# Gate products of a gated hybrid decoder layer as 2 by 2 blocks with seven products

## The chip, the cores and the metric

The kernel runs on one core of a Trainium2 chip. The metric is the device time of one execution in microseconds (us), the median of several runs. TensorE (PE; its weight loads are listed as PEld) multiplies, VectorE is DVE, ScalarE is ACT, GpSimd is POOL, and SyncE (SP) issues most DMAs.

## The reference

One layer of a decoder runs over N = 544 tokens (512 of a prompt, 8 x 4 of samples), with 1024 channels. After a modulated norm, `h` goes through one projection whose columns feed three token mixers and three gates:

```python
h = _rmsnorm(x, lp["norm1_g"]) * (1.0 + sc1) + sh1
z = h @ lp["w_in"]
xa, q, k, v, u, gates = jnp.split(z, list(IN_SPLITS), axis=-1)
...                       # ya: pooling mixer, yb: windowed attention, yc: S5 state space mixer (SSM)
ga, gb, gc = jnp.split(jax.nn.sigmoid(gates), N_BRANCH, axis=-1)
merged = ga * (ya @ lp["w_branch_a"]) + gb * (yb @ lp["w_branch_b"]) + gc * (yc @ lp["w_branch_c"])
x = x + g1 * (merged @ lp["w_out"])
h2 = _rmsnorm(x, lp["norm2_g"]) * (1.0 + sc2) + sh2
a_up, b_up = jnp.split(h2 @ lp["w_ffn_in"], 2, axis=-1)
x = x + g2 * ((jax.nn.silu(a_up) * b_up) @ lp["w_ffn_out"])
```

Each gate is a 1024 by 1024 product. The change concerns the gates `gb` and `gc`.

## The kernel before

All activations lie transposed: a tile holds 128 channels by 544 tokens, so `h` is eight such tiles. Every fp32 operand of a large product is split into a rounded part and a remainder (`hi`, `lo`), and a product is three passes: weight `hi` by `h` hi, weight `hi` by `h` lo, weight `lo` by `h` hi. `quarter` (line 663) splits four weight tiles of 128 x 128 at once: ACT copies into `whi`, DVE subtracts into `wlo`. There are four buffers of each. `gemm` (line 681) runs the three passes for each of the k tiles, each pass as two matmuls of 272 columns (H2 = 272 is half of N).

The three branches follow one another. The eight gate tiles of the first branch are made early (`tgs`, line 763); `mix` (line 1038) multiplies a gate tile by a branch tile's product and adds it to `merged` on POOL for the second and third branch. `branch` (line 1052) does the second and third: for each of four pairs of column tiles it loads 256 gate columns (`load_g`) and 256 branch columns into two of three `raw` buffers, and then does gate, mix, gate, mix; a gate tile is 48 matmuls (`gate`, line 751: 8 k tiles, 3 passes, 2 halves), a mix 24. After the first gate of some pairs comes an `ada` block (line 546), which has two more raw loads of 1 MB, 8 matmuls, a copy and 4 transposes. Between the second and third branch stands the SSM's GLU (line 1079).

The FFN's pairs (`pair`, line 1261) already compute a pair of tiles by a 2 by 2 block scheme: with the weights cut into `a0`, `a1`, `b0`, `b1` (two column tiles by two halves of the channels) and `h2` into halves of channels and of tokens, seven products of 4 k tiles x 3 passes of 272 columns (`product`) replace eight. They need four sums of weight blocks (`s1` to `s4`, tag `ux`) and four sums of blocks of the activation (`T1` to `T4`), which are made once, on DVE and ACT, from the eight `gf` tiles that the FFN's norm leaves. Seven of the sixteen tiles of these sums lie in a large buffer (`tsum`, tag `T`, one buffer), nine in ordinary slots.

That buffer of tag `T` holds first raw weights, then the SSM's taps (`ssm.T`, read by `outputs`), then these sums. Of ordinary slots of 128 x 544 there are 56 (`NS`).

The order of the work is made by a planner (`Program.run`, line 181) before the kernel is built. Each operation has an estimated cost and a priority, which is its place in the program, lowered by a million within `P.high()`. At each moment an engine takes the ready operation of lowest number whose tiles fit (`fits`, line 210: a tile may be taken only if all tiles of lower number that are still to come would have room too). The result is one fixed order for each engine; at run time each engine goes through its own and waits on semaphores.

Of the kernel before, what the change touches and what calls it, by code (L numbers as in the profile page):

```python
# [10 lines left out]
F32 = mybir.dt.float32  # L11
F32R = mybir.dt.float32r
AF = mybir.ActivationFunctionType
OP = mybir.AluOpType
# [416 lines left out]
def body(tc, I, O, dbg=None):  # L431
# [4 lines left out]
    with ExitStack() as ctx:  # L436
# [314 lines left out]
        def gate(b, m, rg):  # L751
            wg = split_w(rg[:, :, 128 * (m % 2):128 * (m % 2) + 128], KT)
            ps = mmt()
            gemm(ps, wg, h1, KT)
            tg = st([128, N], "tg")
            with P.high():
                S.activation(h2v(tg), pv_(ps), AF.Tanh, scale=0.5)
            return tg
# [268 lines left out]
        def split_a(src, name, scale=None):  # L1027
            hi = st([128, N], name + "h", F32R)
            lo = st([128, N], name + "l", F32R)
            if scale is None:  # L1030
                S.copy(hi, src)
                V.tensor_tensor(lo, src, hi.bitcast(F32), op=OP.subtract)
            else:
                S.activation(hi, src, AF.Copy, scale=scale)
                V.scalar_tensor_tensor(lo, src, scale, hi.bitcast(F32), op0=OP.mult, op1=OP.subtract)
            return hi, lo

        def mix(b, m, rb, y, tg):
            wb = split_w(rb[:, :, 128 * (m % 2):128 * (m % 2) + 128], 4)
            ps = mmt()  # L1040
            gemm(ps, wb, y, 4)
            if b == 0:
                mt = st([128, N], "merged")
                merged.append(mt)
            else:
                mt = tg
            with P.high():
                V.scalar_tensor_tensor(h2v(mt), h2v(tg), 1.0, pv_(ps), op0=OP.add, op1=OP.mult)
            if b:
                G.tensor_tensor(merged[m], merged[m], tg, op=OP.add)  # L1050

        def branch(b, y, load, blks):
            for m2 in range(4):
                rg, rb = load_g(b, m2), load(m2)
                for m in (2 * m2, 2 * m2 + 1):
                    tg = gate(b, m, rg)
                    if m == 2 * m2 and m2 < len(blks):
                        ada(blks[m2])
                    mix(b, m, rb, y, tg)

        for m2 in range(4):
            rb = load_w(I["w_branch_a"][0, :, 256 * m2:256 * m2 + 256], 4, 256)
# [3 lines left out]
        def load_b(m2):  # L1066
# [4 lines left out]
                             I["w_branch_b"][0, 256 * h:256 * h + 256, 256 * m2:256 * m2 + 256].rearrange("(k p) n -> p k n", p=64))  # L1071
            return v

        yb = [split_a(ybT[t], "yb") for t in range(4)]
        ssm.stage2()
        branch(1, yb, load_b, (4, 5, 8, 9))


# [171 lines left out]
            V.tensor_tensor(h2v(f), h2v(sg), pv_(pss[1]), op=OP.mult)  # L1250
            return split_a(f, "ff")

        def product(ps, w, act, start):
            for k in range(4):
                (wh, wl), (ah, al) = w[k], act[k]
                with P.unit():
                    for j, (a, b) in enumerate(((wh, ah), (wh, al), (wl, ah))):
                        PE.matmul(ps, a, b, start=start and k == 0 and j == 0, stop=k == 3 and j == 2,
                                  skip_group_check=True)

        def pair(i):

            raw = raw_tile()
            a, b = (raw[:, 1024 * j:1024 * j + 1024].rearrange("p (k n) -> p k n", k=KT) for j in range(2))
            for j, v in enumerate((a, b)):
                c0 = 2816 * j + 128 * i
                SY.dma_start(v, w_ff[:, c0:c0 + 128].rearrange("(k p) n -> p k n", p=128))
            a0, a1, b0, b1 = a[:, 0:4], a[:, 4:8], b[:, 0:4], b[:, 4:8]
            pb, pa_, pd = aux()[:, :H2], mmt()[:, 0, :H2], aux()[:, :H2]
            part, u3, c = st([128, 2, H2], "part"), st([128, 2, H2], "u3"), st([128, N], "ff")  # L1270
            cl, cr = c[:, t0], c[:, t1]
            product(pb, quarter(a0), X00, True)
            with P.high():
                S.copy(part[:, 0], pb)
            product(pa_, quarter(a1), X10, True)
            with P.high():
                V.tensor_tensor(cl, pa_, part[:, 0], op=OP.add)
                S.activation(cl, cl, AF.Silu)
            s1, s2, s3, s4 = (P.tile(up, [128, 4, 128], F32, "ws", "ux", 4) for _ in range(4))
            with P.high():  # L1280
                V.tensor_tensor(s1, b0, b1, op=OP.add)
                V.tensor_tensor(s2, s1, a0, op=OP.subtract)
            product(pb, quarter(s2), T2, False)
            with P.high():
                S.copy(part[:, 1], pb)
            product(pd, quarter(s1), T1, True)
            with P.high():
                V.tensor_tensor(s3, a0, b0, op=OP.subtract)
            product(pb, quarter(s3), T3, False)
            with P.high():  # L1290
                S.copy(u3[:, 0], pb)
                V.tensor_tensor(u3[:, 0], pd, u3[:, 0], op=OP.add)
            product(pb, quarter(b1), T4, False)
            with P.high():
                V.tensor_tensor(s4, a1, s2, op=OP.subtract)
            product(pd, quarter(s4), X11, False)
            with P.high():
                V.tensor_tensor(cr, pd, part[:, 1], op=OP.add)
                V.tensor_tensor(cl, cl, pb, op=OP.mult)
                S.activation(cr, cr, AF.Silu)  # L1300
            V.tensor_tensor(cr, cr, u3[:, 0], op=OP.mult)
            return split_a(c, "ff")

        last = len(PARTS) - 1
        plain = [plain_pair(i) for i in range(2)]


        t0, t1 = slice(0, H2), slice(H2, N)
        room = P.tile(up, [128, 7, N], F32R, "tsum", "T", 1)
        homes = [room[:, i] for i in range(7)]  # L1310

        def home(name):
            return homes.pop() if homes else st([128, N], name, F32R)

        T13, T42 = [], []
        for k in range(4):
          with P.high():
            ga, gb = gfs[k], gfs[k + 4]
            V.tensor_tensor(ga[:, t0], ga[:, t1], ga[:, t0], op=OP.subtract)
            V.tensor_tensor(ga[:, t1], gb[:, t1], ga[:, t1], op=OP.subtract)  # L1320
            V.tensor_tensor(gb[:, t1], gb[:, t1], ga[:, t0], op=OP.subtract)
            V.tensor_tensor(gb[:, t0], gb[:, t0], gb[:, t1], op=OP.subtract)
            for g, dst in ((ga, T13), (gb, T42)):
                hi, lo = home("th"), home("tl")
                S.copy(hi, g)
                V.tensor_tensor(lo, g, hi.bitcast(F32), op=OP.subtract)
                dst.append((hi, lo))
        cols = lambda ps, sl: [(hi[:, sl], lo[:, sl]) for hi, lo in ps]
        X00, X10, X11 = cols(hh[0:4], t0), cols(hh[4:8], t0), cols(hh[4:8], t1)
        T1, T3, T4, T2 = cols(T13, t0), cols(T13, t1), cols(T42, t0), cols(T42, t1)  # L1330

        for part, FH in enumerate(PARTS):
            ff = plain if part == 0 else []
# [458 lines left out]
```

## Time and profile before

| what | value |
|---|---|
| median of 3 runs | 940.92 us (940.81 to 941.09) |
| the profiled execution, in all | 939.36 us |
| its span, first to last instruction | 937.6 us |
| mean granted TensorE clock | 0.988 of full speed |
| instructions in the span | 17684 |
| second branch to the last mix of the third | about 312 to 479 us of the span |
| pairs of the FFN | from about 578 us on, between products of its second matrix |

Times in the rows below are microseconds from the start of the span unless marked ns. In a group of instructions, `out<-in` names the written and read tiles, followed by their shapes, the count, the total busy time and the mean of one. "aux" and "mm" are accumulators in PSUM. In the chain that ended last, each row is a stretch of work that set the end, or the time from it to the next. All lines carry the number of one helper (L426), so tile names tell where a row belongs.

### The profile page before, as it was taken

Reading aid. Unit: us, or ns where it says so; the run is one execution under the profiler, and the core shown is the slowest. Engines: PE = TensorE matmul, PEld = TensorE weight load, DVE = VectorE, ACT = ScalarE, POOL = GpSimd, SP = SyncE. Lnnn points to the kernel's source line nnn. Section 1 sums busy time; section 2 is a strip of 40 time slices with the busy share of each in tenths; the row PEclk is TensorE's granted clock in tenths of the full one; section 3 lists DMA queues with packets and bytes.
Section 4 is the critical chain, followed back from the end, with each engine's and each line's share of the span. In section 5 each row is a group of like instructions: output and inputs, shape, how many; then the busy total and the mean of one; then the engine's idle time right before and its main releaser. Section 6 shows DMA issues by size and latency. Waiting matters only on the chain.

```text
span 937.6 us, 17684 instructions
## 1 busy us (share of the span) xinstructions
PE 895.0 (95%) x7112; PEld 836.6 (89%) x7112; DVE 571.8 (61%) x1226; ACT 409.7 (44%) x871; POOL 105.4 (11%) x126
## 2 busy tenths in 40 slices
PE   2999999999999999999999999999999999999996
PEld 1698998898969998999999879999999999999996
DVE  5468788755663322433336689874578874588743
ACT  6346333345373222332343465652255552155554
POOL 3001000255630011101111100000000000000020
PEclk9799999999998999999999999999999999999998
DMA  9781422600211555544353361323523223432122
GB/s 290 252 258 51 124 79 74 162 24 24 94 30 46 157 158 172 188 157 158 110 190 122 119 166 45 92 63 94 158 80 100 70 67 92 135 92 63 57 63 96
DMA packets 128079, 107.16 MB, mean 114 GB/s; under 512 B 4058, under 2 KB 110942, under 8 KB 127973
## 3 DMA queue, kind: packets, MB, share of 16 engines
q1 hardware_dynamic: 127453, 105.50, 37.5%
q8 instruction: 56, 0.92, 0.4%
q0 software_dynamic: 448, 0.48, 0.3%
q14 instruction: 26, 0.21, 0.1%
q10 hardware_dynamic: 96, 0.04, 0.0%
HBM read 102.39 MB, written 4.81 MB: 114 GB/s over the span
## 4 chain that ended last, share of the span: by engine, by line
PE 82%; DVE 8%; DMA 4%; ACT 3%; issue 1%; SPq 1%; DVEq 0%; ACTq 0%
PE mm L426 55%; PE aux L426 27%; DVE wlo L426 2%; DMA cb<-in_ssm_b_re_dram 1%; ACT whi L426 1%; DVE ffl L426 1%; SPq L426 1%; DVE gf L426 1%; DMA spn<-in_state_pool_dram 1%; DMA xtok<-in_x_prompt_dram 1%; DMA raw<-in_w_ffn_in_dram 1%; DVE Hst L426 0%; DVE rm L426 0%; DVE ws L426 0%; DVE vv L426 0%
## 5 line engine op out<-in xcount | busy, mean ns | idle before, releaser
L426 ACT CAST whi<-raw 128x512 fp32r<-128x512 f32 x224 | 137.2, 614 | 251.0 <-PE mm L426 202.2
L426 DVE TENSOR_TENSOR wlo<-raw,whi 128x512 fp32r<-128x512 f32 x224 | 160.1, 716 | 109.4 <-ACT whi L426 107.2
L426 PE MATMUL mm<-hh,whi 128*128 128x272 f32 x608 | 135.4, 304 | 0.0
L426 PE MATMUL mm<-hl,whi 128*128 128x272 f32 x608 | 126.2, 289 | 0.0
L426 PE MATMUL mm<-hh,wlo 128*128 128x272 f32 x608 | 126.0, 288 | 0.0
L426 PEld LDWEIGHTS mm<-hh,whi 128*128 128x128 f32 x608 | 95.0, 189 | 13.8 <-issue 11.0
L426 PEld LDWEIGHTS mm<-hl,whi 128*128 128x128 f32 x608 | 95.8, 189 | 0.0
L426 PEld LDWEIGHTS mm<-hh,wlo 128*128 128x128 f32 x608 | 95.7, 189 | 0.0
L426 ACT CAST whi<-ws 128x512 fp32r<-128x512 f32 x80 | 48.8, 619 | 66.5 <-PE aux L426 51.1
L426 PE MATMUL mm<-ffh,whi 128*128 128x272 f32 x328 | 68.2, 289 | 0.0
L426 PE MATMUL mm<-ffh,wlo 128*128 128x272 f32 x328 | 67.8, 288 | 0.0
L426 PE MATMUL mm<-ffl,whi 128*128 128x272 f32 x328 | 67.6, 287 | 0.0
L426 POOL TENSOR_TENSOR ssq<-ssq,sq 128x544 f32<-128x544 f32 x10 | 13.6, 1360 | 422.6 <-ACT sq L426 422.6
L426 DVE TENSOR_TENSOR wlo<-ws,whi 128x512 fp32r<-128x512 f32 x80 | 54.4, 687 | 8.5 <-ACT whi L426 5.6
L426 DVE SCALAR_TENSOR_TENSOR xback<-mm,modT,xback 128x272 f32<-128x272 f32 (+3 forms) x64 | 28.4, 478 | 50.8 <-PE mm L426 50.8
L426 PE MATMUL aux<-tsum,whi 128*128 128x272 f32 x280 | 59.2, 292 | 0.0
L426 PE MATMUL aux<-tl,whi 128*128 128x272 f32 x200 | 57.6, 288 | 0.0
L426 PE MATMUL aux<-ghi,wlo 128*128 128x272 f32 x160 | 47.6, 297 | 4.8 <-DVE wlo L426 4.7
L426 PEld LDWEIGHTS mm<-ffl,whi 128*128 128x128 f32 x328 | 51.4, 188 | 0.0
L426 PEld LDWEIGHTS mm<-ffh,wlo 128*128 128x128 f32 x328 | 51.3, 188 | 0.0
L426 PEld LDWEIGHTS mm<-ffh,whi 128*128 128x128 f32 x328 | 51.3, 188 | 0.0
L426 PE MATMUL aux<-ghi,whi 128*128 128x272 f32 x160 | 46.1, 288 | 0.0
(412 smaller groups left out, 2097.2 us busy)
## 6 DMA issues: line engine op xcount, KB each, us to landing
raw<-in_w_ada_dram SPq DMA_DIRECT2D x23, 1024.0 KB, 8.9
raw<-in_w_ffn_in_dram SPq DMA_DIRECT2D x44, 512.0 KB, 4.8
raw<-in_w_in_dram SPq DMA_DIRECT2D x16, 1024.0 KB, 6.4
raw<-in_w_ffn_out_dram SPq DMA_DIRECT2D x16, 512.0 KB, 3.8
raw<-in_w_out_dram SPq DMA_DIRECT2D x4, 1024.0 KB, 5.5
raw<-in_w_ffn_out_dram SPq DMA_DIRECT2D x8, 384.0 KB, 3.5
xtok<-in_x_prompt_dram SPq DMA_DIRECT2D x8, 256.0 KB, 6.5
T<-gd SPq DMA_DIRECT2D x32, 64.0 KB, 3.3
```

The source lines that it names most:

```text
L426: return p.add(tag, cost, lambda: fn(*a, **k), ins, writes, fset, nbytes, after, lock)
```

## The change

In the second and third branch, seven of the eight pairs of gate tiles are computed by the seven products; the first pair of the second branch stays as it was, though its two gates now both come before its two mixes. `product` and the body of `pair` become shared functions (`product`, `seven`), and the sums of the activation a function `sums`, called for `h1` (`XH`, ahead of the second branch, at ordinary priority; it first rebuilds fp32 tiles by adding hi and lo) and for the FFN (`XG`, as before). The sums of `h` take the buffer of tag `T` after the SSM's taps, and nine slots. Each new pair has both gates, then the `ada` block, then both mixes.

```diff
@@ -1052,11 +1052,18 @@
         def branch(b, y, load, blks):
             for m2 in range(4):
                 rg, rb = load_g(b, m2), load(m2)
-                for m in (2 * m2, 2 * m2 + 1):
-                    tg = gate(b, m, rg)
-                    if m == 2 * m2 and m2 < len(blks):
-                        ada(blks[m2])
-                    mix(b, m, rb, y, tg)
+                if b == 1 and m2 == 0:
+                    tg, u3 = gate(b, 0, rg), gate(b, 1, rg)
+                else:
+                    tg, pb, u3 = seven(rg[:, 0:4, 0:128], rg[:, 4:8, 0:128], rg[:, 0:4, 128:256], rg[:, 4:8, 128:256], XH,
+                                       AF.Tanh, 0.5, "tg")
+                    with P.high():
+                        S.activation(u3[:, t0], pb, AF.Tanh, scale=0.5)
+                        S.activation(u3[:, t1], u3[:, t1], AF.Tanh, scale=0.5)
+                if m2 < len(blks):
+                    ada(blks[m2])
+                mix(b, 2 * m2, rb, y, tg)
+                mix(b, 2 * m2 + 1, rb, y, u3)
 
         for m2 in range(4):
             rb = load_w(I["w_branch_a"][0, :, 256 * m2:256 * m2 + 256], 4, 256)
@@ -1071,8 +1078,87 @@
                              I["w_branch_b"][0, 256 * h:256 * h + 256, 256 * m2:256 * m2 + 256].rearrange("(k p) n -> p k n", p=64))
             return v
 
+        t0, t1 = slice(0, H2), slice(H2, N)
+        def sums(full, act):
+            room = P.tile(up, [128, 7, N], F32R, "tsum", "T", 1)
+            homes = [room[:, i] for i in range(7)]
+            def home(name):
+                return homes.pop() if homes else st([128, N], name, F32R)
+            T13, T42 = [], []
+            for k in range(4):
+              with P.shift(0 if full is None else -10 ** 6):
+                if full is None:
+                    ga, gb = (st([128, N], "xsum") for _ in range(2))
+                    for g, (hi, lo) in ((ga, act[k]), (gb, act[k + 4])):
+                        V.tensor_tensor(g, hi.bitcast(F32), lo.bitcast(F32), op=OP.add)
+                else:
+                    ga, gb = full[k], full[k + 4]
+                V.tensor_tensor(ga[:, t0], ga[:, t1], ga[:, t0], op=OP.subtract)
+                V.tensor_tensor(ga[:, t1], gb[:, t1], ga[:, t1], op=OP.subtract)
+                V.tensor_tensor(gb[:, t1], gb[:, t1], ga[:, t0], op=OP.subtract)
+                V.tensor_tensor(gb[:, t0], gb[:, t0], gb[:, t1], op=OP.subtract)
+                for g, dst in ((ga, T13), (gb, T42)):
+                    hi, lo = home("th"), home("tl")
+                    S.copy(hi, g)
+                    V.tensor_tensor(lo, g, hi.bitcast(F32), op=OP.subtract)
+                    dst.append((hi, lo))
+            cols = lambda ps, sl: [(hi[:, sl], lo[:, sl]) for hi, lo in ps]
+            return {"X00": cols(act[0:4], t0), "X10": cols(act[4:8], t0), "X11": cols(act[4:8], t1),
+                    "T1": cols(T13, t0), "T3": cols(T13, t1), "T4": cols(T42, t0), "T2": cols(T42, t1)}
+        def product(ps, w, act, start):
+            for k in range(4):
+                (wh, wl), (ah, al) = w[k], act[k]
+                with P.unit():
+                    for j, (a, b) in enumerate(((wh, ah), (wh, al), (wl, ah))):
+                        PE.matmul(ps, a, b, start=start and k == 0 and j == 0, stop=k == 3 and j == 2,
+                                  skip_group_check=True)
+        def seven(a0, a1, b0, b1, X, func, scale, name):
+            pb, pa_, pd = aux()[:, :H2], mmt()[:, 0, :H2], aux()[:, :H2]
+            part, u3, c = st([128, 2, H2], "part"), st([128, N], "u3"), st([128, N], name)
+            cl, cr, ur = c[:, t0], c[:, t1], u3[:, t1]
+            product(pb, quarter(a0), X["X00"], True)
+            with P.high():
+                S.copy(part[:, 0], pb)
+            product(pa_, quarter(a1), X["X10"], True)
+            with P.high():
+                V.tensor_tensor(cl, pa_, part[:, 0], op=OP.add)
+                S.activation(cl, cl, func, scale=scale)
+            s1, s2, s3, s4 = (P.tile(up, [128, 4, 128], F32, "ws", "ux", 4) for _ in range(4))
+            with P.high():
+                V.tensor_tensor(s1, b0, b1, op=OP.add)
+                V.tensor_tensor(s2, s1, a0, op=OP.subtract)
+            product(pb, quarter(s2), X["T2"], False)
+            with P.high():
+                S.copy(part[:, 1], pb)
+            product(pd, quarter(s1), X["T1"], True)
+            with P.high():
+                V.tensor_tensor(s3, a0, b0, op=OP.subtract)
+            product(pb, quarter(s3), X["T3"], False)
+            with P.high():
+                S.copy(ur, pb)
+                V.tensor_tensor(ur, pd, ur, op=OP.add)
+            product(pb, quarter(b1), X["T4"], False)
+            with P.high():
+                V.tensor_tensor(s4, a1, s2, op=OP.subtract)
+            product(pd, quarter(s4), X["X11"], False)
+            with P.high():
+                V.tensor_tensor(cr, pd, part[:, 1], op=OP.add)
+                S.activation(cr, cr, func, scale=scale)
+            return c, pb, u3
         yb = [split_a(ybT[t], "yb") for t in range(4)]
         ssm.stage2()
+        XH = sums(None, h1)
         branch(1, yb, load_b, (4, 5, 8, 9))
 
 
@@ -1250,14 +1336,6 @@
             V.tensor_tensor(h2v(f), h2v(sg), pv_(pss[1]), op=OP.mult)
             return split_a(f, "ff")
 
...
         def pair(i):
 
             raw = raw_tile()
@@ -1265,69 +1343,16 @@
             for j, v in enumerate((a, b)):
                 c0 = 2816 * j + 128 * i
                 SY.dma_start(v, w_ff[:, c0:c0 + 128].rearrange("(k p) n -> p k n", p=128))
...
+            c, pb, u3 = seven(a[:, 0:4], a[:, 4:8], b[:, 0:4], b[:, 4:8], XG, AF.Silu, 1.0, "ff")
             cl, cr = c[:, t0], c[:, t1]
-            product(pb, quarter(a0), X00, True)
             with P.high():
...
                 V.tensor_tensor(cl, cl, pb, op=OP.mult)
-                S.activation(cr, cr, AF.Silu)
-            V.tensor_tensor(cr, cr, u3[:, 0], op=OP.mult)
+            V.tensor_tensor(cr, cr, u3[:, t1], op=OP.mult)
             return split_a(c, "ff")
 
         last = len(PARTS) - 1
         plain = [plain_pair(i) for i in range(2)]
-
-
...
+        XG = sums(gfs, hh)
 
         for part, FH in enumerate(PARTS):
             ff = plain if part == 0 else []
```

Left out are the lines of `pair` that `seven` now holds word for word, and those of the FFN's sums that `sums` now holds.

## Rows read from the trace of the kernel before

**Rows 1.** The page: busy time by engine; chain that ended last, by engine.
```profile
PE 895.0 (95%) x7112; PEld 836.6 (89%) x7112; DVE 571.8 (61%) x1226; ACT 409.7 (44%) x871; POOL 105.4 (11%) x126
...
PE 82%; DVE 8%; DMA 4%; ACT 3%; issue 1%; SPq 1%; DVEq 0%; ACTq 0%
```

**Rows 2.** Chain that ended last, in the branches: start, length, what.
```profile
333.41 3.20 PE mm L426 x24
...
337.60 1.71 PE mm L426 x12
...
354.32 3.20 PE mm L426 x24
...
435.36 43.74 PE mm L426 x348
```

**Rows 3.** Windows: busy time (instructions) of each engine, granted clock, DMA.
```profile
core 0: us, PE busy (x) PEld busy (x) DVE busy (x) ACT busy (x) POOL busy (x), PEclk, DMA share, GB/s
284.00:292.00 8.00, 8.00 (x51) 7.09 (x50) 0.72 (x1) 1.60 (x7) 0.00 (x0) 0.71 0.00 0
292.00:312.00 20.00, 20.00 (x157) 19.45 (x156) 11.71 (x19) 7.71 (x14) 0.00 (x0) 0.96 0.23 64
312.40:333.40 21.00, 21.00 (x169) 18.99 (x165) 5.93 (x11) 5.31 (x10) 3.04 (x2) 1.00 0.61 178
...
588.85:599.97 11.12, 10.81 (x85) 10.59 (x85) 9.54 (x17) 6.50 (x15) 0.00 (x0) 1.00 0.35 94
```

**Rows 4.** Chain that ended last, in the FFN's pairs.
```profile
588.85 4.53 PE aux L426 x34
...
597.94 0.62 ACT whi L426
...
598.59 0.72 DVE ffl L426
599.31 0.61 DVE wlo L426
...
599.97 4.52 PE aux L426 x34
```

**Rows 5.** Chain that ended last: the product into mm, two FFN pairs apart.
```profile
718.34 1.51 PE mm L426 x12
...
740.76 1.51 PE mm L426 x12
```

**Rows 6.** Groups by shape over the span: busy us, mean ns, idle before.
```profile
L426 DVE TENSOR_TENSOR wlo<-raw,whi 128x512 fp32r<-128x512 f32 x218 | 157.6, 725 | 108.7 <-ACT whi L426 106.5 <-PE aux L426 1.1
...
L426 ACT CAST whi<-raw 128x512 fp32r<-128x512 f32 x218 | 134.8, 619 | 247.1 <-PE mm L426 200.1 <-PE aux L426 23.1 <-ACT part L426 7.5
...
L426 DVE TENSOR_TENSOR wlo<-ws,whi 128x512 fp32r<-128x512 f32 x80 | 54.4, 687 | 8.5 <-ACT whi L426 5.6
...
L426 DVE TENSOR_TENSOR ws<-raw 128x512 f32<-128x512 f32 x40 | 27.3, 689 | 0.8
...
L426 DVE TENSOR_TENSOR ffl<-ff,ffh 128x544 fp32r<-128x544 f32 x22 | 15.8, 719 | 0.1
...
L426 DVE SCALAR_TENSOR_TENSOR tg<-tg,mm 128x544 f32<-128x544 f32 x16 | 11.5, 721 | 39.0 <-PE mm L426 39.0
...
L426 DVE TENSOR_TENSOR ff<-aux,part 128x272 f32<-128x272 f32 x20 | 8.7, 436 | 1.5 <-PE aux L426 1.5
```

**Rows 7.** Matmuls on the taps: ns min/median/max, first and last start.
```profile
L426 PE MATMUL aux<-T,U x64: 272/273/273, 124.0 to 189.1; 128*72 128x128 f32 x64
```

**Rows 8.** SP's queue in the second branch, in order of time.
```profile
330.56 0.37 SPq L426 DMA_DIRECT2D raw<-in_w_ada_dram  x1
333.47 0.37 SPq L426 DMA_DIRECT2D raw<-in_w_in_dram  x1
```

**Rows 9.** POOL in order of time, around 379.
```profile
379.32 1.35 POOL L426 TENSOR_TENSOR merged<-merged,tg 128x544 f32<-128x544 f32 x1 [8.50 <-DVE tg L426]
```

**Rows 10.** DVE in order of time, around 379.
```profile
379.62 1.61 DVE L426 TENSOR_TENSOR wlo<-raw,whi 128x512 fp32r<-128x512 f32 x1 [0.38 <-ACT whi L426]
```

More of the change, by code (lines that the diff above doesn't have):

```diff
@@ L1251, in plain_pair @@
             return split_a(f, "ff")
[L1253 to L1259, printed above, removed]
         def pair(i):
@@ L1267, in pair @@
                 SY.dma_start(v, w_ff[:, c0:c0 + 128].rearrange("(k p) n -> p k n", p=128))
-            a0, a1, b0, b1 = a[:, 0:4], a[:, 4:8], b[:, 0:4], b[:, 4:8]
-            pb, pa_, pd = aux()[:, :H2], mmt()[:, 0, :H2], aux()[:, :H2]
-            part, u3, c = st([128, 2, H2], "part"), st([128, 2, H2], "u3"), st([128, N], "ff")
+            c, pb, u3 = seven(a[:, 0:4], a[:, 4:8], b[:, 0:4], b[:, 4:8], XG, AF.Silu, 1.0, "ff")
             cl, cr = c[:, t0], c[:, t1]
-            product(pb, quarter(a0), X00, True)
             with P.high():
[L1274 to L1298, printed above, removed]
                 V.tensor_tensor(cl, cl, pb, op=OP.mult)
-                S.activation(cr, cr, AF.Silu)
-            V.tensor_tensor(cr, cr, u3[:, 0], op=OP.mult)
+            V.tensor_tensor(cr, cr, u3[:, t1], op=OP.mult)
             return split_a(c, "ff")
@@ L1305, in body @@
         plain = [plain_pair(i) for i in range(2)]
[L1308 to L1330, printed above, removed]
+        XG = sums(gfs, hh)
         for part, FH in enumerate(PARTS):
```

## The prediction

> **What bounds the kernel now.** I read the page's busy shares first and then the chain that ended last [rows 1]: TensorE is busy for 95% of the span and carries 82% of the chain. A busy TensorE proves little by itself, so the next view is the chain in the stretch that the change touches, the second and third branch [rows 2]. There the chain is TensorE without a hole. Its last unbroken piece holds 348 matmuls of 272 columns in 43.74 us, 43.74 / 348 = 0.1257 us each. From 333.41 to 354.32 one turn of the second branch (two gate tiles of 48 matmuls, two mixes of 24, one `ada` block) takes 20.91 us; 144 x 0.1257 = 18.10, so the `ada` block costs 2.81 and nothing is left for waiting. The windows [rows 3] show the other engines in the same stretch: DVE 5.93 of 21.0 us, ACT 5.31, POOL 3.04, and the granted clock at 1.00, its upper level of 2.4 GHz. So a matmul that is left out here is worth its 0.1257 us, if the weights and sums that replace it come in time.
>
> The nearest thing to the new code runs already: the FFN's pairs do the same seven products. Their chain [rows 4] shows what that costs. A pair has 7 x 12 = 84 matmuls, 84 x 0.1257 = 10.56 us, but comes every 11.12 us (588.85 to 599.97). The missing 0.56 is one chain per pair: a weight buffer comes free, ACT makes `whi`, DVE finishes an `ffl`, then makes `wlo`, and only then does the next product go on. Later in the FFN two pairs take 740.76 - 718.34 = 22.42 us [rows 5], a loss of 22.42 / 2 - 10.56 = 0.65 each. In that stage DVE is 86% busy (9.54 of 11.12) [rows 3].
>
> **The change, part by part.**
>
> *Matmuls removed.* Seven pairs of gate tiles go from 96 to 84 matmuls of the same width and the same count of passes: 7 x 12 = 84 fewer, 84 x 0.1257 = -10.56 us. Nothing is added on TensorE; the mixes, the `ada` blocks and the loads have the same sizes.
>
> *DVE work added in a pair* [rows 6]. Three more `wlo` (0.73 from raw, 0.69 from sums), four weight sums `ws` at 0.69, and three adds out of PSUM at 0.44. The whole of DVE in a new pair: 3 x 0.73 + 4 x 0.69 for `wlo`, 4 x 0.69 for `ws`, 3 x 0.44, two `wlo` (1.45) and two `tg` (1.44) of the mixes: 11.9 us, with the `mgl` of the third branch (priced as an `ffl`, 0.72) 13.4. TensorE's part of that pair is 84 + 48 = 132 matmuls, 16.6 us, and 19.4 with an `ada` block. So DVE stays below TensorE as a mean, at 72 to 81% without the `ada`, a little under the FFN's 86%.
>
> *ACT work added.* Three more `whi` at 0.62, three copies and four half activations in place of two full ones. ACT was busy for 5.31 of 21.0 us; twice that is still under two thirds. I cost it at nothing; it counts only as the first link of the FFN's stall.
>
> *The stall inside a pair.* The third product into `pb` must be copied out by ACT before the fourth may go on adding to it, and the next weight buffer is freed late, as in the FFN. Something else must fill TensorE there. Where an `ada` block lies behind the pair (five of the seven), its matmuls read raw weights and need no split, so they can fill it; in the other two the first mix has to, and its `wlo` comes by the same route as in the FFN. From below the stall is 0 (the gate stretch today has none), from above 0.65 (the FFN). I take 0.64 for the two and 0.15 for the five, nearer to zero because no `ffl` stands ahead of `wlo` and a filler exists: 2 x 0.64 + 5 x 0.15 = +2.0 us. Bounds 0 and 7 x 0.65 = 4.6.
>
> *The sums of h.* `sums(None, h1)` costs DVE 8 adds of 544 columns, 16 of 272 and 8 `lo` of 544: 8 x 0.72 + 16 x 0.44 + 8 x 0.72 = 18.6 us [rows 6], and ACT 8 copies. The first pair that uses them is the second of branch two, around 333, and its first two products need no sum. Their big buffer is the one of the SSM's taps, whose last reader runs at 189.1 [rows 7]. What holds them back are the 56 slots: by my count of the tiles alive they fit once the first branch's tiles go, from some point between 285 and 296. DVE has room from there: 7.3 free of 8 us (284 to 292), 8.3 of 20, and 12.0 of 21 in the untouched first pair even after POOL's 3.04 is taken off as if it blocked DVE [rows 3]. That is 27.6 us for 18.6, so most is hidden; I put +0.3. If the cover before 312 were gone, 18.6 - 12.0 = 6.6 would show; with no cover at all, 18.6.
>
> *Slots.* Nine slots stay taken through both branches: 16 (h) + 8 (merged) + 8 + 4 + 9 = 45 of 56. A pair needs three and `ada` one, so pairs still run. Splits for the GLU, now made early, must wait for the end of branch two. They are off the chain, and the next gate needs none of them; 0, at most 8 `lo` at 0.72 = 5.8 if TensorE had to stand behind them.
>
> *Loads.* The gate's raw tile is held until the last weight sum, some 8 us into the pair, and both mixes come after it. Today one raw buffer of the three is handed on just in time: `w_in` is issued at 333.47 [rows 8], after the first half of the `ada` block, and its gate runs from 337.60, covered by one mix and half an `ada`, some 4 us. After the change two mixes (6.0 us) lie in that place. I cost it at 0.
>
> *FFN.* The same products through the shared function; one multiply is issued after an activation instead of before it: 0.
>
> Sum against the profiled execution (span 937.6, 939.36 in all, that is 1.76 around the span): 939.36 - 10.56 + 2.0 + 0.3 = 931.1 us. The median of the runs is 940.92, 1.56 above that execution, so the forecast is 932.6 us; its own range, with stalls from 0 to 3.5 and the sums at up to 0.5, is 930.4 to 934.4.
>
> **One rule against it.** When POOL's add of `merged` ran from 379.32 for 1.35 us, a `wlo` that began at 379.62 took 1.61 us instead of 0.69 [rows 9, 10]. The Trainium skill (SBUF — State Buffer, "SBUF: two separate sides") says that a DVE instruction with two SBUF inputs and a GpSimd instruction share a port pair that whoever starts first locks for its whole length; the trace agrees. `wlo` and `ws` are of that kind, and there are more of them now: by that rule the fourteen adds of the seven pairs could hold DVE for 14 x 1.35 = 18.9 us, where the sum above goes by today's chain, in which the blocked `wlo` cost TensorE nothing, and puts 0.
>
> **Rivals.**
> - *A, the FFN's stall everywhere.* Seven times 0.65, with 1 to 2 us of the sums showing because DVE runs them beside the splits. For it: the same function, the same four weight buffers. Against: 48 of the 132 matmuls of a pair are mixes, in which DVE has little to do. 940.92 - 10.56 + 4.6 + 1 to 2 = 936 to 937.
> - *B, POOL's adds stop the splits.* Two adds per pair now follow each other within 3 us of mixes, just when the next pair's first weights are split. If one add of 1.35 per pair shows on TensorE: 932.6 + 7 x 1.35 = 942.1, no change. With 11.9 + 2 x 1.35 = 14.6 of 16.6 us (16.1 in the third branch) DVE would nearly be the bound. Against: today the same blockings cost TensorE nothing.
> - *C, slower: the sums are not covered.* The third product of the first new pair needs all four tiles of T2. If the slots let the sums begin only behind the untouched pair, 18.6 us stand open: 932.3 + 18.6 = 950.9. It decides from 8.6 us in the open (940.92 - 932.3).
> - That the change removes less than it says is ruled out by the counts: every product is 12 matmuls of 272 columns.
>
> **How the numbers follow.** Forecast 0.60, A 0.21, B 0.08, C 0.09; 0.02 is left for something not seen. A measurement of this kernel tells about 0.2%, 1.9 us, from no change. The forecast and A are faster: 0.81. B and a C just at its point are the same: 0.09; slower 0.10. The range runs from no stall at all (930.4, with the scatter of the runs 930.2) to A's end with some of the slots' cost, 937.8; it holds the forecast and A.
>
> **What the profile would show.** TensorE has 7028 matmul records, DVE some 100 more (70 in the pairs, 32 in the sums), ACT some 64 more. The chain between 312 and the output projection stays TensorE, with holes of 0.3 to 0.6 us in the pairs without `ada`, released by DVE `wlo`; wide holes in every pair speak for A, holes behind `wlo` of 1.3 us or more beside POOL for B. The `th` and `tl` sums are done before about 336; a TensorE hole there, released by DVE, is C. The stretch from 312.5 to 479.1 shrinks by 8 us, and everything after it, the FFN above all, keeps its length. I am wrong if a stage outside the branches moves by more than 1 us: then the order of the plan, not this sum, decided.

## The result and the profile after

The changed kernel takes 934.33 us (median of five runs, 932.29 to 935.95) against 940.92 before on the same chip: a ratio of 0.9935, 95% interval 0.9915 to 0.9954, that is 6.1 us faster with an interval of 4.3 to 8.0. On another chip it was 935.05 against 940.63, 0.9942 (0.9923 to 0.9961), 5.5 us. The forecast of 932.6 was 1.7 to 2.5 us too low; the range of 930.2 to 937.8 held it. The profiled execution took 935.95 us (span 934.0), the longest of its five.

First, the page: busy time by engine, and the chain that ended last by engine.

```profile
PE 889.2 (95%) x7028; PEld 828.5 (89%) x7028; DVE 634.8 (68%) x1328; ACT 435.3 (47%) x935; POOL 107.8 (12%) x126
...
PE 82%; DVE 7%; DMA 5%; ACT 4%; SPq 1%; issue 1%; DVEq 0%; ACTq 0%
```

Against [rows 1], 84 matmuls are gone and 102 DVE and 64 ACT instructions have come, as forecast. TensorE's share of the chain is unchanged. What is new is DMA with 5% for 4%, in a kernel that loads nothing more.

To see where the time went I cut each span at points that every variant has, all read from matmuls of one kind: the first on `yah` (begin of the branches' mixes), the last on `yah` (the first branch is done), the first on `xagain` (the last mix is done, output projection), `ghi` on `wth` (begin of the FFN), `ffh` on `whi` (first product with the FFN's second matrix) and `ffh` on `wth` (its last part), to the end of the span. "Branches" runs from the first `yah` to `xagain`; "behind yah" is the part of it that follows the last `yah`. In us:

```
                                  branches  behind yah  out. projection  FFN, begin  FFN, rest  tail
before                              227.6      173.8          57.5           96.1       281.7    23.3
after                               219.7      163.5          59.4           97.2       282.1    23.2
after, other chip                   219.6      163.3          59.1           97.2       282.1    23.3
order alone (e1)                    228.2      172.0          57.4           96.0       282.0    23.3
nine slots held (e2)                230.0      173.8          57.6           96.0       282.1    23.4
second branch only (e3)             224.8      168.8          57.4           96.4       281.9    23.3
third branch only (e4)              221.7      168.0          58.6           97.2       282.1    23.3
half of x in a raw tile (e7)        217.0      163.3          57.6           97.4       282.0    23.2
  the same, other chip              218.1      163.3          57.6           97.2       282.0    23.3
before, half of x in raw (e7b)      230.0      173.8          57.4           95.9       282.5    23.4
w_out loads behind x (e9)           219.8      163.7          57.5           97.2       282.0    23.5
sums twice on DVE (e6)              232.6      176.3          59.4           97.2       281.9    23.3
all eight pairs (e5)                234.0      169.9          60.4           97.0       281.8    23.3
```

So the branches gave 7.9 us, and two stages that the sum had at nothing took 3.0 back. What lies ahead of the branches differs by up to 4 us from profile to profile (250.3 to 254.6 us, with the time at which the first taps have landed), whatever the variant; I read nothing from it.

**The granted clock in the branches' first part.** These are windows of after (busy us of each engine with its instructions, granted clock, DMA's share, GB/s); the first two lie in the first branch, whose matmuls the change leaves as they were, the last covers a new pair of the second.

```profile
core 0: us, PE busy (x) PEld busy (x) DVE busy (x) ACT busy (x) POOL busy (x), PEclk, DMA share, GB/s
284.00:288.00 4.00, 4.00 (x18) 3.54 (x18) 0.82 (x2) 0.41 (x2) 0.00 (x0) 0.50 0.00 0
288.00:292.00 4.00, 4.00 (x26) 3.41 (x24) 0.00 (x0) 0.00 (x0) 0.00 (x0) 0.50 0.00 0
...
332.50:351.90 19.40, 19.40 (x154) 17.43 (x154) 12.08 (x19) 9.72 (x20) 3.43 (x2) 1.00 0.64 191
```

From 284 to 292 the granted clock is 0.50, the lower level of 1.2 GHz, where [rows 3] has 0.71; the matmuls there are the same ones in the same order. Summing (1 - granted clock) x 4 us over 276 to 304 gives 6.8 us lost after and 3.4 before. But e2 and e7b, whose branches hold before's work, lost 6.8 as well and took 230.0 us; e4 lost 3.4, and the same kernel e7 lost 3.4 in one profile and 5.1 in another. It is an execution's luck, worth 230.0 - 227.6 = 2.4 us in this stretch. The unprofiled runs of before on the second chip show as much: five at a mean granted clock of 0.988 took 938.8 us on average, six at 0.984 took 941.0. Against e2 and e7b, which have after's clock, after's branches gave 230.0 - 219.65 = 10.35 us. The part behind `yah`, where the granted clock is 1.00 in before and after alike, says the same without them: 173.8 in before, e2 and e7b, 163.5 and 163.3 after.

**The pairs.** The chain that ended last, in after (start, length, what):

```profile
342.94 1.72 PE mm L426 x12
...
357.46 0.95 PE mm L426 x6
...
362.39 1.70 PE mm L426 x12
...
440.16 1.51 PE mm L426 x12
...
446.15 0.62 ACT whi L426
446.78 0.29 ACT u L426
...
447.11 3.27 PE aux L426 x24
...
457.16 1.51 PE mm L426 x12
...
467.02 8.49 DMA xagain<-in_x_prompt_dram
```

One new pair with its `ada` block and two mixes takes 362.39 - 342.94 = 19.45 us; before it was 20.91 [rows 2]. The chain there is TensorE alone, but not at its full rate: the six mix matmuls at 357.46, which stand where the copy out of `pb` is awaited, take 0.95 us for 6 x 0.1257 = 0.75. At 446.1 the chain leaves TensorE inside a pair, the only time between 300 and 466: the fourth product into `pb` waits for ACT to copy the third one out (`u`), and that copy stood behind a `whi`. The last line is new and belongs to the output projection.

### The profile page after: what moved, and what is told of

Same layout as the page of the kernel before. It is cut to its first block, busy times and chain, and to the rows that moved or that the text cites. A ratio compares the mean times of both kernels' runs of the same rounds, so it can differ in the third digit from the quotient of the medians.

```text
span 934.0 us, 17715 instructions
## 1 busy us (share of the span) xinstructions
PE 889.2 (95%) x7028; PEld 828.5 (89%) x7028; DVE 634.8 (68%) x1328; ACT 435.3 (47%) x935; POOL 107.8 (12%) x126
## 4 chain that ended last, share of the span: by engine, by line
PE 82%; DVE 7%; DMA 5%; ACT 4%; SPq 1%; issue 1%; DVEq 0%; ACTq 0%
PE mm L426 47%; PE aux L426 35%; ACT whi L426 2%; DMA cb<-in_ssm_b_re_dram 2%; DVE wlo L426 1%; DVE ffl L426 1%; SPq L426 1%; DMA xtok<-in_x_prompt_dram 1%; DMA xagain<-in_x_prompt_dram 1%; DMA spn<-in_state_pool_dram 1%; DVE gf L426 1%; DMA raw<-in_w_ffn_in_dram 1%; DVE Hst L426 0%; DVE rm L426 0%; DVE vv L426 0%
## 5 line engine op out<-in xcount | busy, mean ns | idle before, releaser
L426 ACT CAST whi<-raw 128x512 fp32r<-128x512 f32 (+1 forms) x217 | 132.4, 614 | 189.4 <-PE mm L426 134.7
L426 DVE TENSOR_TENSOR wlo<-raw,whi 128x512 fp32r<-128x512 f32 (+1 forms) x217 | 153.7, 714 | 71.3 <-ACT whi L426 68.9
L426 PE MATMUL mm<-hh,whi 128*128 128x272 f32 x412 | 95.9, 308 | 0.0
L426 PE MATMUL mm<-hl,whi 128*128 128x272 f32 x412 | 87.7, 289 | 0.0
L426 PE MATMUL mm<-hh,wlo 128*128 128x272 f32 x412 | 87.7, 289 | 0.0
L426 PEld LDWEIGHTS mm<-hl,whi 128*128 128x128 f32 x412 | 65.7, 189 | 0.0
L426 PE MATMUL aux<-th,whi 128*128 128x272 f32 x216 | 62.2, 288 | 0.0
L426 PEld LDWEIGHTS aux<-tsum,whi 128*128 128x128 f32 x378 | 60.6, 188 | 1.8 <-ACT part L426 1.1
L426 PE MATMUL aux<-th,wlo 128*128 128x272 f32 x216 | 62.1, 288 | 0.0
L426 PE MATMUL aux<-tsum,wlo 128*128 128x272 f32 x216 | 62.1, 287 | 0.0
```

The source lines that it names most:

```text
L426: return p.add(tag, cost, lambda: fn(*a, **k), ins, writes, fset, nbytes, after, lock)
```

## The experiments

**Order alone** (e1), on the kernel before:

```diff
-                for m in (2 * m2, 2 * m2 + 1):
-                    tg = gate(b, m, rg)
-                    if m == 2 * m2 and m2 < len(blks):
-                        ada(blks[m2])
-                    mix(b, m, rb, y, tg)
+                tg, u3 = gate(b, 2 * m2, rg), gate(b, 2 * m2 + 1, rg)
+                if m2 < len(blks):
+                    ada(blks[m2])
+                mix(b, 2 * m2, rb, y, tg)
+                mix(b, 2 * m2 + 1, rb, y, u3)
```

> The kernel before, with the order of the changed one alone: both gates of a pair, the ada block, both mixes; all gates plain, no sums. My account puts this at nothing: within 1 us of the kernel before, and the FFN stage as long as there. If two mixes in a row make TensorE wait for POOL's adds or the loads, it shows as holes in the pairs.

Measured: 939.08 against 941.42, 0.998 (0.9966 to 0.9994), and 228.2 us in the branches against 230.0 at the same clock: 1.8 us faster, where I had expected at most 1 us either way. Its chain (start, length, what):

```profile
340.35 1.85 PE aux L426 x16
342.20 1.70 PE mm L426 x12
343.89 0.44 PE aux L426 x4
344.33 16.59 PE mm L426 x132
360.92 1.85 PE aux L426 x16
362.77 1.70 PE mm L426 x12
```

A turn is 362.77 - 342.20 = 20.57 us, 0.34 less than 20.91. The `ada` block's matmuls (16 records), which ran before in two pieces with a gate's matmuls between them, now run as one in 1.85 us, so the block costs 20.57 - 18.10 = 2.47 instead of 2.81. A turn of the third branch gains less, 20.89 (412.32 to 433.21) to 20.65 (415.93 to 436.58). Four blocks at 0.34 and two at 0.24 make the 1.8 that the stretch shows. The prediction had taken the order for free; it is a gain of its own, independent of the seven products.

**Nine slots held** (e2), on the kernel before: nine tiles written ahead of the second branch and read at the end of the third.

```diff
+        held = [st([128, N], "held") for _ in range(9)]
+        for t in held:
+            V.memset(t[:, 0:1], 0.0)
         branch(1, yb, load_b, (4, 5, 8, 9))
...
                     tg = gate(b, m, rg)
+                    if b == 2 and m == 7:
+                        for t in held:
+                            V.tensor_tensor(tg[:, 0:1], tg[:, 0:1], t[:, 0:1], op=OP.add)
```

> The kernel before, all gates as they were, plus nine slots taken ahead of the second branch by one-column memsets and let go in the last gate of the third (nine one-column adds on the gate tile, which change that column's value by zero). Theory S (slots): the nine slots that the sums hold keep the second load of x from being issued early, so TensorE waits for it at the output projection; here that appears without any seven products: 1.4 to 2 us slower than the kernel before, the issues of xagain end under 5 us before the last mix of the third branch (7 us in the kernel before) and TensorE has holes of about 1.4 us at its transposes. Rival P (pairs): the missing part of the gain is lost inside the new pairs; then this kernel is as fast as the kernel before within 0.5 us.

Measured: 941.64 against 941.44, 1.0005 (0.9994 to 1.0016). My first theory, that the sums' nine slots hold back the tiles of x and so lengthen the output projection, fell: that stage took 57.6 us. SP's queue in time order:

```profile
467.23 2.81 SPq L426 DMA_DIRECT2D raw<-in_w_out_dram  x2
470.09 1.03 SPq L426 DMA_DIRECT2D xagain<-in_x_sample_dram  x2
471.16 6.23 SPq L426 DMA_DIRECT2D xagain<-in_x_prompt_dram  x8
```

With the slots taken, all of x is issued late here, up to 477.4, and still the transposes, from 480.5 on, wait for nothing: the planner put matmuls on `mgh` between them there (482.06 and 483.57), so most are due later.

**One branch at a time** (e3: three pairs of the second branch; e4: four pairs of the third; the others are plain gates in the new order), by the condition in `branch`:

```diff
-                if b == 1 and m2 == 0:
+                if b == 2 or m2 == 0:      # e3
+                if b == 1:                 # e4
```

> Only the three pairs of the second branch use seven products; the third branch is plain, so the sums of h and their nine slots are let go 80 us before x is loaded again. Theory S: 3 x 12 x 0.1257 = 4.5 us faster and no hole at xagain, a total of 4 to 4.5 us. Rival P, with the measured 6.1 us of seven pairs spread evenly: 3/7 x 6.1 = 2.6 us.

> Only the four pairs of the third branch use seven products. The sums and their slots are held as in the changed kernel. Theory S: 4 x 12 x 0.1257 = 6.0 us less the wait for x of 1.4 to 1.9 us, 4.1 to 4.6 us faster, with the hole at xagain. Rival P: 4/7 x 6.1 = 3.5 us.

Measured: e3 936.45 against 941.44, 0.9953 (0.9941 to 0.9966), 4.4 us faster; e4 937.4, 0.9959 (0.9947 to 0.9972), 3.9 us faster. Both contain the 1.8 us of the order, so together they give 4.4 + 3.9 - 1.8 = 6.5, near the whole change's 5.5 to 6.1. In e3's branches, 36 fewer matmuls (-4.53), the order (-1.8) and three stalls of 0.39 (below) make -5.2, and the stretch shows 224.8 - 230.0 = -5.2. In e4 the like sum is -6.7 and the stretch 221.7 - 227.6 = -5.9. Of the 0.8 between them, 0.5 is a wait of TensorE for ACT's copy `part` at 428.5, in a new pair, which after does not have; the rest I can't place. The two differ in the stages behind: e3 pays 0.3 at most there, e4 1.1 in the output projection and 1.1 in the FFN's begin. So the cost behind the branches comes with the third branch's pairs.

**Whose fault is the output projection?** In after, SP's queue in time order:

```profile
447.71 13.25 SPq L426 DMA_DIRECT2D raw<-in_w_out_dram  x2
461.01 1.03 SPq L426 DMA_DIRECT2D xagain<-in_x_sample_dram  x2
462.08 1.37 SPq L426 DMA_DIRECT2D xagain<-in_x_prompt_dram  x3
464.53 0.38 SPq L426 DMA_DIRECT2D raw<-in_w_out_dram  x1
465.01 3.62 SPq L426 DMA_DIRECT2D xagain<-in_x_prompt_dram  x5
```

What SP's queue waited for from 440 to 480 (us in total, times, longest):

```profile
SPq L426 <- DVE wlo L426: 27.6, 3, 12.4
```

And TensorE from 471 on (in brackets its idle time and the releaser):

```profile
472.14 1.04 PE L426 MATMUL aux<-ca,xagain 32*128 32x32 f32 x10
474.26 0.98 PE L426 MATMUL aux<-ca,xagain 128*128 128x128 f32 x7 [1.07 <-DMA xagain<-in_x_prompt_dram]
475.56 0.99 PE L426 MATMUL aux<-ca,xagain 128*128 128x128 f32 x7 [0.32 <-DMA xagain<-in_x_prompt_dram]
```

The second load of `w_out` needs a raw buffer, which comes free only when a gate's last `wlo` has read it; it waits up to 12.4 us, and the ten loads of x stand behind it in the same queue. Their own tiles come free earlier: in e9 below, with the same slots taken, all ten are issued by 456.8. They go out from 461.0 to 468.6, the last lands at 467.02 + 8.49 = 475.5, and TensorE waits 1.07 + 0.32 = 1.4 us. Before, the queue did the same:

```profile
450.07 0.38 SPq L426 DMA_DIRECT2D raw<-in_w_out_dram  x1
450.50 1.19 SPq L426 DMA_DIRECT2D xagain<-in_x_sample_dram  x2
451.74 0.42 SPq L426 DMA_DIRECT2D xagain<-in_x_prompt_dram  x1
465.73 2.82 SPq L426 DMA_DIRECT2D raw<-in_w_out_dram  x2
468.60 3.42 SPq L426 DMA_DIRECT2D xagain<-in_x_prompt_dram  x7
```

There the last x was issued at 472.0 and the transposes began at 479.0, 7.0 us later. After, the branches end at 472.1, 3.5 us behind the last issue. The loads moved by 3.4 us, the work that needs them by 6.9, and no matmul on `mgh` stands between the transposes before 476.3. Two edits take this cause away in two ways. e7 puts half of x into a raw buffer, ahead of the `w_out` loads:

```diff
         xo = {}
+        xr = raw_tile()
...
-                xo[t, h] = st([128, 512], "xagain")
+                if h == 0 and t < 4:
+                    xo[t, h] = xr[:, 512 * t:512 * t + 512]
+                else:
+                    xo[t, h] = st([128, 512], "xagain")
```

> The changed kernel, with the first half of x (four of the ten tiles that are loaded again) in one of the three raw buffers instead of in four slots. Theory S: these loads are no longer held back by the slots, they are issued some 15 us earlier, the hole of 1.4 us at the transposes goes, and the kernel is 1 to 2 us faster than the changed kernel: 7 to 8.5 us faster than the kernel before. Rival P: no change against the changed kernel, 6 us faster than the kernel before.

> The version with half of x in a raw buffer once more, since its first runs were few. By the stretches of its profile it should be 1.8 us faster than the changed kernel and 8 to 9.5 us faster than the kernel before; the 10 us of the first runs would then hold some luck with the granted clock around 285 us.

and e7b makes the same edit on the kernel before:

> The kernel before with the first half of x in a raw buffer. There TensorE did not wait for x, so by theory S nothing is to be gained: within 0.7 us of the kernel before. If the raw buffer itself helps or hurts (the output projection's weights wait for it), it shows here.

e9 keeps the buffers and lets the second to fourth `w_out` load wait until x has landed:

```diff
-                SY.dma_start(xo[t, h][:rows], src[:, 512 * h:512 * h + 512])
+                xlast = SY.dma_start(xo[t, h][:rows], src[:, 512 * h:512 * h + 512])
...
-            rw = load_w(I["w_out"][0, :, 256 * m2:256 * m2 + 256], KT, 256)
+            rw = load_w(I["w_out"][0, :, 256 * m2:256 * m2 + 256], KT, 256, [xlast] if m2 else ())
```

> The changed kernel with the second to fourth weight loads of the output projection (1 MB each, two of them issued just ahead of and between the loads of x) made to wait until x has landed. Theory Q (queue): x is late because these loads are served ahead of it and between its parts; then x lands earlier, the hole of 1.4 us at the transposes closes, and from the last mix to the FFN takes 57.6 us instead of 59.4. Theory S (slots): x is late because its slots come free late; then it is issued at the same times, most of the hole stays, and that stretch takes about 59 us.

Measured: e7 931.08 against 941.44, 0.9889 (0.9875 to 0.9902), and again 932.18 against 941.42, 0.991 (0.9889 to 0.9932); e9 931.59, 0.9902 (0.9884 to 0.9919); e7b 941.76 against 940.63, 1.0007 (0.9994 to 1.002). e9's SP queue, and then its TensorE:

```profile
446.72 1.76 SPq L426 DMA_DIRECT2D xagain<-in_x_sample_dram  x2
448.93 7.90 SPq L426 DMA_DIRECT2D xagain<-in_x_prompt_dram  x8
458.63 13.58 SPq L426 DMA_DIRECT2D raw<-in_w_out_dram  x3
```

```profile
470.19 3.45 PE L426 MATMUL aux<-ca,xagain 32*128 32x32 f32 x32
```

x is issued by 456.8 and the transposes run without a hole. The output projection is back at 57.5 and 57.6 us in both variants, with the nine slots still taken, while e7b shows that before had nothing to gain there. So the queue's order is the cause, and the slots are not. Whether x is late only because it is issued late, or also because `w_out` moves beside it, these two edits don't tell apart. e7's 10.4 us is more than the 7 to 8.5 expected at first; the 9.2 of its second runs lies within the 8 to 9.5 expected then.

**The cover of the sums.** e5 drops the untouched pair (all eight by seven products), e6 lets DVE do its part of the sums twice, the second time into tiles that nobody reads:

```diff
-                if b == 1 and m2 == 0:
+                if False:                  # e5
...
+                if full is None:           # e6
+                    da, db = (st([128, N], "xtwice") for _ in range(2))
+                    for g, (hi, lo) in ((da, act[k]), (db, act[k + 4])):
+                        V.tensor_tensor(g, hi.bitcast(F32), lo.bitcast(F32), op=OP.add)
+                    ...   # the four subtractions of halves, and two more of full width
```

> All eight pairs use seven products, so that the plain pair that covered the sums is gone. If the cover counted (the sums are ready at about 321, the third product of the first pair would run at about 312): the pair saves another 1.5 us and TensorE waits up to 8 us for the sums, 0 to 6 us slower than the changed kernel. If the order of the plan moves mixes or other work ahead, or if the sums come earlier by themselves: 1 to 1.5 us faster than the changed kernel.

> The changed kernel with DVE's part of the sums of h done twice (a second, unused copy: 8 adds, 16 and 8 subtractions, some 18.6 us more on DVE, and two more slots while each lasts). My account had 27.6 us of room for 18.6; 37.2 then leave 9.6 us too many. Theory: the first new pair waits, 5 to 10 us slower than the changed kernel. Rival, that DVE's room is larger, because the pair stage leaves some and the order lets first products and mixes run: less than 3 us slower.

Measured: e5 950.42 against 940.63, 1.0104 (1.0081 to 1.0127), some 15 us slower than after, far beyond the 6 that I had put as its worst; e6 947.05, 1.0075 (1.0057 to 1.0092), 12 us slower than after, a little above the 5 to 10 expected. In after, the sums on DVE in time order, the first and the last:

```profile
282.00 0.72 DVE L426 TENSOR_TENSOR xsum<-hh,hl 128x544 f32<-128x544 f32 x1
...
319.08 1.52 DVE L426 TENSOR_TENSOR tl<-xsum,th 128x544 fp32r<-128x544 f32 x2
```

They run from 282 to 320.6, and the first products on them follow at about 332: nothing shows. With twice the work, e6's windows, and then its TensorE, are

```profile
312.00:324.00 12.00, 12.00 (x98) 10.41 (x98) 12.00 (x24) 4.67 (x8) 0.00 (x0) 1.00 0.56 169
...
342.00:348.00 6.00, 1.50 (x5) 1.18 (x5) 5.87 (x15) 2.17 (x4) 0.00 (x0) 0.50 0.28 66
```

```profile
332.35 1.07 PE L426 MATMUL aux<-raw,cT 128*32 128x512 f32 x8
...
337.87 1.94 PE L426 MATMUL aux<-raw,cT 128*32 128x512 f32 x8
...
345.74 0.59 PE L426 MATMUL aux<-tl,whi 128*128 128x272 f32 x1 [3.85 <-DVE tl L426]
```

DVE is full, then TensorE idles for 4.5 of 6 us, and the granted clock falls to 0.50 behind the first holes. The branches are 232.6 - 219.6 = 13.0 us longer. TensorE's waits from 332 to 348 make 8.2 of that (6.0 for DVE's `tl`); the rest is work at the lower clock. So, by an estimate from these numbers, 9 to 10 of the 18.6 us of added work were hidden; the prediction's count had left room for 27.6 - 18.6 = 9.0.

e5 loses in two places. The first lies ahead of the sums: from the first to the last `yah` matmul it takes 64.1 us (234.0 - 169.9) where after takes 56.2. DVE, then TensorE, then a window there:

```profile
258.48 1.28 DVE L426 TENSOR_TENSOR ws<-raw 128x512 f32<-128x512 f32 x2
...
262.48 0.69 PE L426 MATMUL aux<-ca,sc 128*128 128x128 f32 x2 [2.69 <-POOL sc L426]
...
268.00:272.00 4.00, 4.00 (x13) 2.73 (x12) 2.07 (x5) 2.15 (x8) 0.22 (x1) 0.50 0.00 0
```

The first pair's gate weights are here by then, and DVE makes its four weight sums (`ws`, within `P.high()`) and a `wlo` from 258.5 to 261.5, in the middle of the first branch's attention. A small operation on `den` waits behind them (in after it follows at once), POOL's `sc` waits for `den`, TensorE 2.7 us for `sc`, and the granted clock then stands at 0.50 up to 276. The second place is behind `yah`: 169.9 us where after takes 163.5, though 12 matmuls (1.5 us) are gone. Its windows, and then its chain:

```profile
318.00:324.00 6.00, 3.75 (x23) 2.02 (x22) 5.90 (x13) 2.31 (x4) 0.00 (x0) 0.93 0.58 189
324.00:330.00 6.00, 5.40 (x15) 1.83 (x15) 4.79 (x10) 1.91 (x3) 0.00 (x0) 0.50 0.50 162
```

```profile
319.34 5.21 DMA raw<-in_w_ada_dram
...
324.60 5.46 PE aux L426 x14
```

Without the cover TensorE waits 1.9 us for the sums (`th`, `tl`) and 1.0 us for the next `ada` load, whose raw buffer is handed on late, and goes on at a granted clock of 0.50 until 330. So each place costs some 8 us, the clock's fall included, against the 1.5 saved: one is the missing cover, the other the weight sums in the attention's way, a thing of the planned order that no run here tries by itself. Rival C's 950.9 is near e5's time by chance: C had 18.6 us of sums in the open, and the waits for sums here are 1.9.

**After once more**, as the partner of e5, e6 and e7b on their chip:

> The changed kernel once more, beside the experiments. Theory K (clock): part of the gain that is missing in its profiled run, about 2 us, lies between 280 and 297 us, where the granted clock fell to half for longer than in the kernel before although TensorE's work there is the same; if that is chance, this profile shows another length of that stretch, and the gain in the runs varies by 2 us. Rival O (order): the new order lengthens it, and this profile shows the same stretch again.

It gave 935.05, the second figure at the head of this part. Its stretch lost 6.8 us again, as O has it; but e2 and e7b lose as much in before's order, and e7 less in the new one, so the order isn't the cause, and K holds.

## Why the prediction was right, and where it was off

- *Matmuls removed, -10.56.* Right. At the same clock the branches gave 10.35, which is -10.56, -1.8 for the order and +2.0 for stalls. The order's 1.8 is no term of the sum; that the forecast held is in part luck, since this gain made up for more than half of what the stages behind lost.
- *The stall inside a pair, +2.0.* Right in sum, wrong in its parts. A pair with an `ada` block takes 19.45 in the second branch, where TensorE's work is 16.59 + 2.47 = 19.06, and 19.37 in the third, where it is 16.59 + 2.55 = 19.14: 0.4 three times and 0.2 twice, instead of 0.15. Of the two pairs without one, the one around 446 lost 0.4 (457.16 - 440.16 = 17.00 for 16.59 of work) and the other nothing, instead of 0.64 twice. The filler was mostly a mix, not the `ada` block. The releaser was ACT's copy, not DVE's `wlo`. Rival A's 0.65 in every pair is not there.
- *POOL's adds (rival B), 0.* Right. After, the sixteen adds take 1.65 to 1.86 us each, and TensorE waits for nothing from 308 to 471. The 1.35 of [rows 9] was the short kind: before had six of 1.35 to 1.36 and ten of 1.66 to 1.74, and e1, in the new order alone, has only long ones too. The Trainium skill (SBUF — State Buffer, "SBUF: two separate sides") has DVE and GpSimd lock each other out of a shared port pair. The trace agrees: before's add at 327.35 began within a `wlo` (from 327.13) and took 1.67, the one at 316.68 began with DVE idle and took 1.36. Its cost for the kernel stays nil as long as the split weights are there early.
- *The sums of h, +0.3.* Right: done by 320.6, used from 332. e6 bears out the room's size to within 1 us or so, but not its place: of the 7.3 us free between 284 and 292 the sums took 0.8, and none ran from 284.8 to 301.7.
- *Loads, 0.* This is the step that failed. It looked only at the gate's raw tile and at who waits for it on TensorE. It did not look at what stands behind that wait in SP's queue: the loads of x, which serve the next stage. The output projection grew by 1.9 us (59.4), and both edits that free x give it back.
- *Slots, 0.* Right by e2, though the tiles of x are among those that they hold back.
- *FFN, 0.* Off by 1.1 us in its begin. TensorE waits there once for 0.9 us, for ACT; after's chain:

```profile
567.63 0.60 ACT whi L426
568.23 0.29 ACT part L426
568.52 0.04 issue
568.57 3.53 PE aux L426 x26
```

  Before has no wait for `part` in this stretch, and neither has e3, which runs the same shared functions (96.4 us); e4 has one of 0.6. So it isn't the function. That it is an order which the planner chose behind the third branch's new pairs is likely but not shown, and its cause stays open. That a stage outside the branches moved by over 1 us is what the prediction named as a sign that the plan's order decided; in the output projection's 1.9 us it did.

The shown parts add up to -10.35 + 1.8 (the mean of 1.9 and 1.6) + 1.1 = -7.4 at the same clock; the timed difference is -6.1 (-8.0 to -4.3) and -5.5 (-7.2 to -3.7). The first interval holds it and the second ends just short of it. Compared at one mean granted clock, the runs give 6.4 on the first chip (0.988: 939.36 once before, 933.0 twice after) and 6.9 on the second (0.985: 940.9 and 934.0, twice each). What is left, 0.5 to 1.0 us, I can't place.

**A version that beats both** is e7 or e9: 931.1 to 932.2 us, some 9 to 10 us under before and about 3 under after by medians. The profiles show 1.8 of these 3, the hole at x. e7's first interval (up to 0.9902) lies clear of after's (from 0.9915); its second (up to 0.9932) and e9's (up to 0.9919) reach into it.

## What to carry to other kernels

When a stage gets shorter, follow its DMA queue into the next stage: a load whose buffer isn't free holds back every load behind it, and loads that were early enough before are late by what the stage has gained. Put loads with free tiles ahead of those that wait, or behind an explicit dependence. And measure cover before spending it: seven pairs of eight gained 6 us, and the eighth, which would save another 1.5 us of matmuls, cost 15, about half because the sums had hidden behind it and half because its own weight sums, put ahead by their priority, got in the way of the stage before.

## What the runs showed of the hardware

The granted clock was not the same for the same matmuls in the same order: 3.4, 5.1 or 6.8 us lost between 276 and 304 from one profile to the next, with the branches longer by 2.4 us at the two ends. And holes cost more than their length: in e5 and e6 the granted clock stood at 0.50, the lower level, right behind them. In e6 eight matmul records of an `ada` block took 1.94 us there, where eight had taken 1.07 at 1.00 before the holes; e5's 2.7 us of waiting at 260 was followed by some 12 us at 0.50, and its first branch became 7.9 us longer.

In before, POOL's adds and DVE's operations on two SBUF tiles held each other up in both directions: a `wlo` took 1.61 us instead of 0.69 behind an add [rows 9, 10], and an add 1.67 instead of 1.36 behind a `wlo`.
